# A two-layer MoE backbone: the selection of further blocks cut into pieces, and the first block without a list written as straight code under a condition

## The chip, the cores and the metric

The kernel runs on one core of a Trainium2 chip, as one launch. The metric is device time in microseconds (us) of a whole execution. TensorE is called PE here, its weight loads PEld, VectorE DVE, ScalarE ACT, GpSimd POOL, and SyncE, which issues nearly all weight loads, SP.

## What is computed

A backbone of two layers over 512 latent tokens of 1024 numbers with 256 context tokens beside them. Layer 0 mixes tokens by latent attention, layer 1 by a short gated convolution; a mixture of experts (MoE) follows each. Its core, cut to what matters:

```python
# 32 experts in 4 groups, 2 experts a token, 512 hidden numbers an expert
g_sel  = argmax(softmax(h @ w_group) + b_group)               # a group for each token
top_idx = top_k(softmax(logits of the group) + bias, 2)       # two experts in it
...
yp = lax.map(expert_block, (blocks of tokens of one expert, their expert))
def expert_block(xb, e):
    return (silu(xb @ w_gate[e]) * (xb @ w_up[e])) @ w_down[e]
return segment_sum(yp[dest] * weight, token)
```

How many tokens an expert gets depends on the data. All weights are fp32 and come from HBM: 6 MB an expert, 32 experts, two layers.

## The kernel before, in words

`moe()` (L583) runs once for each layer. Tokens are handled in blocks of 64 (`SLOTS`). There are 36 `LISTS`: the first 64 tokens of each of the 32 experts, and `FURTHER` = 4 further blocks, the next 64 tokens of those experts that have more than 64. Which expert a further block belongs to is known only at run time. `count_further()` (L711) counts on DVE how many further blocks each expert has (`nov`), where its first one stands (`first`), and their sum (`novi`); `select()` (L728) finds for `n` further blocks the expert (`own`, an integer that SP reads later), the place of each token in the block (`pos`) and three columns of its routing weight (`r`). Blocks beyond those four are handled by `beyond()` (L758): a loop `For_i(FURTHER, nv)` (L764) whose bounds every engine reads from memory. In this data it runs once in layer 0 and not at all in layer 1.

An expert `e` is, on PE: `gate_up` (L658, 32 matmuls, all of 64 tokens), the transposes `h_T` (L671), `down` (L681, 16 matmuls). Between the matmuls of `gate_up` stand the matmuls of `combine` (L698) of the expert before: eight of them, each followed by an add on DVE into the token tiles (L700). `fetch` (L642) transposes token rows of a later pair of experts there too. On the other engines: silu on ACT (L664) and times up on DVE (L665); `weighted` (L684) multiplies the expert's output by the routing weight on DVE (L686), makes the one-hot matrix `ohs` (L690), and splits the product into a high part (ACT, L688 and L689) and a low part (POOL L691, DVE L692). `combine` multiplies these with `ohs`. The rows of a block come by an indirect DMA on POOL (L635), from row numbers that a small matmul (L620, `table`) picks with a one-hot tile `pt` (L608, `onehot`); for the lists this is done for a pair of experts, two pairs ahead.

Each engine goes through its own instructions in program order, and the order follows the loop over `e` at L839. SP issues the loads in that order too: four blocks of gate and up weights (L302, 1 MB each) run 13 blocks ahead, the two `down` blocks (L315, 1 MB each) three experts ahead, and each load waits until its buffer is free. After expert 34 and before expert 35 the kernel combines expert 34 in one go and calls `beyond()`; expert 35 has no combine within it. `ahead(0..2)` issue the loads of the convolution's weights (L1527) in layer 0.

Of the kernel before, what the change touches and what calls it, by code (L numbers as in the profile page):

```python
# [87 lines left out]
def backbone(ctx: ExitStack, tc: tile.TileContext, A, out):  # L88
# [494 lines left out]
    def moe(l, x, big, normed, weights, gain, start, step, ahead=lambda i: None):  # L583


        with ExitStack() as st:
# [123 lines left out]

            def count_further():  # L711

                th = wide_[:, 256:256 + STEPS]
                cmp = wide_[:, :EXPERTS * STEPS].rearrange("p (e s) -> p e s", s=STEPS)
                dve.tensor_scalar(th, iota[:, :STEPS], float(SLOTS), float(SLOTS), op0=ALU.mult, op1=ALU.add)
                dve.tensor_tensor(cmp, cnt.unsqueeze(2).to_broadcast([P, EXPERTS, STEPS]),
                                  th.unsqueeze(1).to_broadcast([P, EXPERTS, STEPS]), op=ALU.is_gt)
                dve.memset(sc[:, 32:128], 0.0)
                dve.tensor_reduce(nov, cmp, axis=AX, op=ALU.add)
# [1 line left out]
                dve.tensor_copy(a[:, 16:], nov)
                for d in (1, 2, 4, 8, 16):
                    dve.tensor_add(b[:, 16:], a[:, 16:], a[:, 16 - d:48 - d])
                    a, b = b, a
                dve.tensor_sub(first, a[:, 16:], nov)
                dve.tensor_copy(novi, a[:1, 47:48])

            def select(ks, n, pos, r, own):  # L728


                d = sc[:, 160:160 + n * EXPERTS].rearrange("p (k e) -> p k e", e=EXPERTS)
                m = wide_[:, 256:256 + n * EXPERTS].rearrange("p (k e) -> p k e", e=EXPERTS)
                f = sc[:, 224:224 + n]
                prod = wide_[:, :4 * n * EXPERTS].rearrange("p (t k e) -> p t k e", t=4, e=EXPERTS)
                full = [P, n, EXPERTS]
                dve.tensor_tensor(d, ks.unsqueeze(2).to_broadcast(full), first.unsqueeze(1).to_broadcast(full), op=ALU.subtract)
                dve.tensor_tensor(m, d, nov.unsqueeze(1).to_broadcast(full), op=ALU.is_lt)
                dve.scalar_tensor_tensor(m, d, 0.0, m, op0=ALU.is_ge, op1=ALU.mult)
                dve.tensor_mul(d, d, m)
                dve.tensor_reduce(f, d, axis=AX, op=ALU.add)  # L740
                dve.tensor_scalar(f, f, float(SLOTS), SLOTS + 1.0, op0=ALU.mult, op1=ALU.add)
                dve.tensor_mul(d, m, iota[:, :EXPERTS].unsqueeze(1).to_broadcast(full))
                g = sc[:, 228:228 + n]
                dve.tensor_reduce(g, d, axis=AX, op=ALU.add)
                dve.tensor_copy(own, g[:1])
                for t in range(4):
                    dve.scalar_tensor_tensor(prod[:, t], posm[:, t, :].unsqueeze(1).to_broadcast(full), 1.0, m,
                                             op0=ALU.add, op1=ALU.mult)
                dve.tensor_reduce(pos, prod, axis=AX, op=ALU.add)
                for t in range(4):  # L750
                    dve.tensor_sub(pos[:, t], pos[:, t], f)
                for c in range(2, NTAB):
                    for t in range(4):
                        dve.tensor_mul(prod[:, t], R[:, t, :, c].unsqueeze(1).to_broadcast(full), m)
                    dve.tensor_reduce(g4 := sc[:, 160:160 + 4 * n].rearrange("p (t k) -> p t k", t=4), prod, axis=AX, op=ALU.add)
                    dve.tensor_copy(r[:, :, :, c], g4)

            def beyond():  # L758

                k, pos = cur[:, :1], cur[:, 4:8].rearrange("p (t k) -> p t k", k=1)  # L760
                dve.memset(k, FURTHER - 1.0)
                dve.tensor_copy(rc[:, :, 0], R[:, :, 0])
                nv = nc.values_load(novi[0:1, 0:1], min_val=0, max_val=2 * STEPS)
                with tc.For_i(FURTHER, nv, 1):  # L764
                    e = LISTS
                    dve.tensor_scalar_add(k, k, 1.0)
                    select(k, 1, pos, rc, owner[:, FURTHER:])
                    whose[l, e] = nc.values_load(owner[0:1, FURTHER:FURTHER + 1], engines=(mybir.EngineType.SP,),
                                                 min_val=0, max_val=EXPERTS - 1)
                    for i in range(4):  # L770
                        gate_block(l, e, i, big(f"gx{l}_{i}"))
                    load_down(l, e, big)
                    pt = onehot(pos, 0, 1, "x")
                    table(pt, rc, 1, LISTS, "x")
                    gather(LISTS // 2, (LISTS, LISTS), xgs[0])
                    v = xgs[0].rearrange("s (p j) -> s j p", j=8)
                    xTo = wide_.rearrange("p (j s) -> p j s", s=SLOTS)
                    for h in range(2):
                        tx = psum.tile([P, 4, SLOTS], F32, tag=("o", "xt")[h], name=f"tx{l}_{h}")
                        for j in range(4):  # L780
                            pe.transpose(tx[:, j], v[:64, 4 * h + j, :], ident[:64, :64])
                        for j in range(4):
                            act.activation(xTo[:, 4 * h + j, :], tx[:, j], AF.Identity, bias=mcol[:, l, 3, 0, 4 * h + j:4 * h + j + 1],
                                           scale=mcol[:, l, 4, 0, 4 * h + j:4 * h + j + 1])
                    gu = psum.tile([P, 512], F32, tag="gu", name=f"gux{l}")
                    gate_up(xTo, e, gu, {})
                    h_T("x")
                    y = psum.tile([P, 512], F32, tag="y", name=f"yx{l}")
                    down(e, y)
# [918 lines left out]
```

## Time and profile before

| what | us |
|---|---|
| three runs | 1911.83, 1905.15, 1909.97 |
| their median | 1909.97 |
| the profiled execution, whole | 1906.3 |
| its span (first to last instruction) | 1904.5 |
| mean clock granted to PE in it, as a share of full speed | 0.951 |
| DVE busy | 1151.3 |
| ACT busy | 580.6 |
| POOL busy | 368.3 |

The span lies 1.8 us below the time of the same execution, and that execution 3.7 us below the median of the runs. Times within the execution are counted from the span's start. "Layer 0" in what follows is its MoE, roughly 440 to 1050 us, and "layer 1" its MoE, roughly 1320 to 1895 us.

### The profile page before, as it was taken

The numbers are of one execution on the slowest core, as the hardware profiler recorded it, in microseconds if no ns is written. First come the engines' busy times: TensorE is split into PE (matmuls) and PEld (weight loads), VectorE is DVE, ScalarE is ACT, GpSimd is POOL, SyncE is SP. The second block draws the span as 40 slices with busy tenths as digits, with TensorE's granted clock in tenths as the row PEclk, the third lists the DMA queues.
The fourth block names the chain that finished last, engine by engine and source line by source line (L and its number), as shares of the span: only waits on it lengthen the run. The fifth ranks groups of instructions, "written<-read, shape, count | busy, mean of one in ns | idle before, by whom it ended". The sixth has DMA issues, their size and how long they took to land. (4 is left out here: it accounts for less than half of the span.)

```text
span 1904.5 us, 23932 instructions
## 1 busy us (share of the span) xinstructions
PE 1740.9 (91%) x8686; PEld 928.5 (49%) x8686; DVE 1151.3 (60%) x2339; ACT 580.6 (30%) x1329; POOL 368.3 (19%) x308
## 2 busy tenths in 40 slices
PE   5989999998889999999967999997988999999995
PEld 2878887863333333333322888873333333333331
DVE  4767787564665566555552776644666655566554
ACT  3455655221212222222211422222212222222222
POOL 0436666200100111101100321210101010111101
PEclk9999999998989999999987999998999999999996
DMA  9124334578989999999973473458999999999991
GB/s 342 55 99 153 130 120 155 208 310 313 417 334 410 417 417 416 416 416 417 416 296 146 146 247 108 133 205 327 417 364 359 416 416 417 416 417 416 417 382 56
DMA packets 139703, 574.24 MB, mean 302 GB/s; under 512 B 21184, under 2 KB 23488, under 8 KB 100928
## 3 DMA queue, kind: packets, MB, share of 16 engines
q1 hardware_dynamic: 132816, 549.09, 73.2%
q0 software_dynamic: 5328, 19.40, 2.6%
q10 hardware_dynamic: 1440, 4.20, 0.6%
q8 instruction: 70, 1.15, 0.2%
q14 instruction: 49, 0.40, 0.1%
HBM read 566.36 MB, written 6.29 MB: 301 GB/s over the span
## 5 line engine op out<-in xcount | busy, mean ns | idle before, releaser
L658 PE MATMUL gu<-gu,mA 128*64 128x512 f32 x2304 | 553.9, 614 | 3.5 <-issue 2.1
L700 DVE TENSOR_TENSOR xb<-xb,c 128x512 f32<-128x512 f32 x576 | 362.7, 682 | 61.0 <-PE c L698 58.1
L658 PEld LDWEIGHTS gu<-gu,mA 128*64 128x64 f32 x2304 | 154.4, 140 | 293.3 <-issue 290.8
L691 POOL TENSOR_TENSOR yst<-mB,yst 64x512 fp32r<-64x512 f32 x70 | 88.5, 1265 | 918.9 <-ACT yst L688 918.9
L681 PE MATMUL y<-d,mB 128*64 128x512 f32 x1152 | 263.1, 598 | 0.0
L698 PE MATMUL c<-yst,ohs 128*128 128x512 f32 x576 | 222.0, 468 | 34.3 <-DVE xb L700 23.2
L664 ACT ACTIVATE mB<-gu 64x256 f32<-64x256 f32 x144 | 54.4, 377 | 612.0 <-PE gu L658 576.7
L698 PEld LDWEIGHTS c<-yst,ohs 128*128 128x128 f32 x576 | 102.0, 195 | 171.9 <-DVE xb L700 89.9
L686 DVE SCALAR_TENSOR_TENSOR mB<-y,tab,mB 128x512 f32<-128x512 f32 x72 | 54.1, 751 | 204.6 <-PE y L681 204.6
L665 DVE TENSOR_TENSOR mB<-mB,gu 64x256 f32<-64x256 f32 x144 | 60.9, 423 | 144.0 <-ACT mB L664 144.0
L681 PEld LDWEIGHTS y<-d,mB 128*64 128x64 f32 x1152 | 76.3, 136 | 128.2 <-issue 123.3
L692 DVE TENSOR_TENSOR yst<-mB,yst 64x512 fp32r<-64x512 f32 x73 | 91.8, 1258 | 65.3 <-ACT yst L689 64.3
L647 ACT ACTIVATE mA<-xt,mcol 128x128 f32<-128x128 f32 x280 | 105.5, 457 | 24.1 <-issue 22.4
L688 ACT CAST yst<-mB 64x512 fp32r<-64x512 f32 x73 | 45.2, 620 | 196.4 <-DVE mB L686 196.4
L113 PE MATMUL bcu<-a1H,wis 128*128 128x512 f32 (+1 forms) x216 | 83.1, 385 | 0.0
L114 PE MATMUL bcu<-a1L,wis 128*128 128x512 f32 (+1 forms) x216 | 82.2, 381 | 0.0
L115 PE MATMUL bcu<-a1H,wis 128*128 128x512 f32 (+1 forms) x216 | 82.1, 380 | 0.0
L642 PEld LDWEIGHTS xt<-kc,xg 128*128 128x128 f32 x288 | 38.9, 196 | 73.5 <-issue 58.9
L671 PE MATMUL htp<-kc,mB 64*128 64x64 f32 x288 | 46.1, 240 | 28.2 <-DVE mB L665 19.3
L635 POOL DMA_INDIRECT xg<-normed,rows x37 | 36.1, 975 | 177.3 <-DVE rows L634 73.3
L109 POOL TENSOR_TENSOR wis<-wi,wis 128x512 fp32r<-128x512 f32 x26 | 39.6, 1531 | 151.6 <-ACT wis L108 149.0
L642 PE MATMUL xt<-kc,xg 128*128 128x128 f32 x288 | 52.9, 310 | 13.7 <-DMA xg<-normed,rows 13.7
(544 smaller groups left out, 2616.8 us busy)
## 6 DMA issues: line engine op xcount, KB each, us to landing
d<-in_moe_w_down_dram SPq DMA_DIRECT2D x146, 1024.0 KB, 14.4
gu<-in_moe_w_gate_dram SPq DMA_DIRECT2D x144, 1024.0 KB, 15.3
gu<-in_moe_w_up_dram SPq DMA_DIRECT2D x144, 1024.0 KB, 13.5
wm<-in_w_mod_dram SPq DMA_DIRECT2D x48, 1024.0 KB, 6.1
wi<-in_conv_w_in_dram SPq DMA_DIRECT2D x12, 1024.0 KB, 7.2
wo<-in_mla_w_o_dram SPq DMA_DIRECT2D x4, 1024.0 KB, 6.5
normed<-xn ACTq DMA_DIRECT2D x8, 512.0 KB, 4.7
wo<-in_conv_w_out_dram SPq DMA_DIRECT2D x4, 1024.0 KB, 5.0
```

The lines of the kernel that those rows point to most:

```text
L113: pe.matmul(o, ah, bh, start=first, stop=False)
L114: pe.matmul(o, ah, bl, start=False, stop=False)
L115: pe.matmul(o, al, bh, start=False, stop=last)
L642: pe.transpose(xt[:, j - js[0], :], v[:, j, :], ident)
L647: act.activation(xTs[b % 2][:, j], xt[:, j - js[0], :], AF.Identity, bias=mcol[:, l, 3, 0, j:j + 1], scale=mcol[:, l, 4, 0, j:j + 1])
L658: pe.matmul(gu[64 * s:64 * s + 64, :], xT[:, j, :], gates[l, e, j // 4 * 2 + s][:, j % 4, :], start=j == 0, stop=j == 7, tile_position=(0, ...
L665: dve.tensor_mul(ys[:64, cs], ys[:64, cs], gu[64:, cs])
L681: pe.matmul(y[64 * h:64 * h + 64, :], hT[:, k * 64:(k + 1) * 64], d[k // 2][:, k % 2, 512 * h:512 * h + 512], start=k == 0, stop=k == 3, t ...
L691: lo_engine.tensor_sub(y0[64:], ys[:64], y0[:64].bitcast(F32))
L692: dve.tensor_sub(y1[:64], ys[64:], y1[64:].bitcast(F32))
L698: pe.matmul(cps, ohs[:, t * P:(t + 1) * P], yst[:, h], start=True, stop=True)
L700: dve.tensor_add(xs, xs, cps)
```

## The change

- The selection is cut into 17 pieces: `counted` and `placed` (from `count_further`), then five pieces of `select` for each pair of further blocks and for one block more, the first without a list. Each expert from 2 to 18 runs one of them, after its combine and before its `down`.
- That one block more (number `FURTHER`) is selected always. Its expert is read by SP at `e` = 26, its row table and gather are made at `e` = 32 (`next_rows("a")`), and its 6 MB of weights are loaded at `e` = 33 (`next_weights`), in both layers and whether it has tokens or not.
- `beyond()` now tests `nv > FURTHER` (L818 of the changed kernel). Under the condition stands `block("a")`: the combine of expert 34, the block's transposes, `gate_up`, `h_T`, `down` and `weighted`. A loop for still further blocks follows within the condition, with the selection and loads of each as before.
- The combine of the last of these (or of expert 34, if the condition fails) is done within expert 35, as in every other expert.
- `ahead(0)` and `ahead(1)` move by one place each.

The diff, with the bodies that only got a name left out:

```diff
             def count_further():
...
+                return [counted, placed]
             def select(ks, n, pos, r, own):
...
+                def which():
...
+                def places():
...
+                def part(c):
...
+                return [which, places] + [lambda c=c: part(c) for c in range(2, NTAB)]
+
+            kx, posn = cur[:, :1], cur[:, 4:8].rearrange("p (t k) -> p t k", k=1)
+
+            def next_block():
+                return select(kx, 1, posn, rc, owner[:, FURTHER:])
+
+            def next_expert():
+                whose[l, LISTS] = nc.values_load(owner[0:1, FURTHER:FURTHER + 1], engines=(mybir.EngineType.SP,),
+                                                 min_val=0, max_val=EXPERTS - 1)
+            spare = []
+
+            def next_weights():
+                for i in range(4):
+                    gate_block(l, LISTS, i, spare[i])
+                left = spare[4:]
+                load_down(l, LISTS, lambda name: left.pop(0))
+
+            def next_rows(tag):
+                table(onehot(posn, 0, 1, tag), rc, 1, LISTS, tag)
+                gather(LISTS // 2, (LISTS, LISTS), xgs[0])
+
+            def block(tag):
+                combine(range(8), f"x{tag}")
...
+                weighted(y, tab[:, LISTS], dve)
 
             def beyond():
...
-                with tc.For_i(FURTHER, nv, 1):
...
-                    weighted(y, tab[:, LISTS], dve)
-                    combine(range(8), "x")
+                with tc.If(nv > FURTHER):
+                    block("a")
+                    with tc.For_i(FURTHER + 1, nv, 1):
+                        dve.tensor_scalar_add(kx, kx, 1.0)
+                        for f in next_block():
+                            f()
+                        next_expert()
+                        next_weights()
+                        next_rows("x")
+                        block("b")
...
-                if 0 < e < LISTS - 1:
+                if e:
                     between[3] = lambda: combine(range(3), f"{e - 1}")
...
-                within = 0 < e < LISTS - 1
+                within = e > 0
...
                 evac()
+                if e > 1 and few:
+                    few.pop(0)()
                 down(e, y)
 
+            few = count_further()
+            for k in range(0, FURTHER, 2):
+                ks = slice(k, k + 2)
+                few += select(iota[:, ks], 2, posx[:, :, ks], Rx[:, :, ks], owner[:, ks])
+            dve.memset(kx, float(FURTHER))
+            dve.tensor_copy(rc[:, :, 0], R[:, :, 0])
+            few += next_block()
             for e in range(LISTS):
...
-                if e == 2:
-                    count_further()
-                    dve.tensor_copy(Rx[:, :, :, :2], R[:, :, :FURTHER, :2])
-                if e in (4, 6):
-                    ks = slice(e - 4, e - 2)
-                    select(iota[:, ks], 2, posx[:, :, ks], Rx[:, :, ks], owner[:, ks])
...
+                    next_expert()
+                if e == LISTS - 4:
+                    next_rows("a")
                 if e == LISTS - 2:
-                    combine(range(8), e)
+                    ahead(0)
                     beyond()
+                    ahead(1)
...
-                if LISTS - 3 <= e < LISTS - 1:
-                    ahead(e - LISTS + 3)
+                if e == LISTS - 3:
+                    for i in range(4):
+                        spare.append(big(f"gx{l}_{i}") if i < 2 else ozblk(f"gx{l}_{i}", F32))
+                    spare.extend(wblk(f"dx{l}_{h}") for h in range(2))
+                    next_weights()
```

DVE at expert 4 of layer 0. Before (`xb` are the token tiles, `c0_3` the combine of expert 3, `y0_4` the output of expert 4, `mB` a tile that holds scratch):

```order
L700 TENSOR_TENSOR xb1_3290<-xb1_3290,c0_3_7_4452 128x512
L686 SCALAR_TENSOR_TENSOR mB0_3874<-y0_4_4398,tab0_3877,mB0_3874 128x512
L690 TENSOR_SCALAR ohs0_3876<-kc_86,tab0_3877 128x512
L692 TENSOR_TENSOR yst0_3875<-mB0_3874,yst0_3875 64x512
L624 TENSOR_REDUCE tab0_3877<-tb0_b4c0_4476 128x2
L625 TENSOR_SCALAR tab0_3877<-tab0_3877 128x2
L627 TENSOR_REDUCE tab0_3877<-tb0_b4c0_4476 128x2
L634 TENSOR_SCALAR rows0_3878<-tab0_3877 64x1 x2
L736 TENSOR_TENSOR mB0_3874<-kc_86,mB0_3874 128x64
```

and in the changed kernel:

```order
L700 TENSOR_TENSOR xb1_3290<-xb1_3290,c0_3_7_4454 128x512
L748 TENSOR_TENSOR mB0_3874<-kc_86,mB0_3874 128x64
L749 TENSOR_TENSOR mB0_3874<-mB0_3874 128x64
L750 SCALAR_TENSOR_TENSOR mB0_3874<-mB0_3874 128x64
L751 TENSOR_TENSOR mB0_3874<-mB0_3874 128x64
L752 TENSOR_REDUCE mB0_3874<-mB0_3874 128x2
L753 TENSOR_SCALAR mB0_3874<-mB0_3874 128x2
L754 TENSOR_TENSOR mB0_3874<-mB0_3874,kc_86 128x64
L755 TENSOR_REDUCE mB0_3874<-mB0_3874 128x2
L756 CAST owner0_3884<-mB0_3874 1x2
L686 SCALAR_TENSOR_TENSOR mB0_3874<-y0_4_4400,tab0_3877,mB0_3874 128x512
L690 TENSOR_SCALAR ohs0_3876<-kc_86,tab0_3877 128x512
```

The selection began (L736) behind `weighted` of expert 4 and went on with all its instructions; now the first piece, `which`, stands between the last add of the combine and `weighted`, and the other pieces are with later experts.

DVE at expert 32 of layer 0. Before:

```order
L686 SCALAR_TENSOR_TENSOR mB0_3874<-y0_32_7324,tab0_3877,mB0_3874 128x512
L690 TENSOR_SCALAR ohs0_3876<-kc_86,tab0_3877 128x512
L692 TENSOR_TENSOR yst0_3875<-mB0_3874,yst0_3875 64x512
L700 TENSOR_TENSOR xb0_3289<-xb0_3289,c0_32_0_7416 128x512
L700 TENSOR_TENSOR xb0_3289<-xb0_3289,c0_32_1_7419 128x512
```

and in the changed kernel (`pt0_a` is the one-hot tile, `tb0_a` the table that PE makes from it, right behind the `down` of expert 32 and ahead of the `gate_up` of expert 33):

```order
L686 SCALAR_TENSOR_TENSOR mB0_3874<-y0_32_7372,tab0_3877,mB0_3874 128x512
L690 TENSOR_SCALAR ohs0_3876<-kc_86,tab0_3877 128x512
L692 TENSOR_TENSOR yst0_3875<-mB0_3874,yst0_3875 64x512
L608 TENSOR_TENSOR pt0_a_7448<-cur0_3880,kc_86 128x256
L624 TENSOR_REDUCE tab0_3877<-tb0_a_7450 128x1
L625 TENSOR_SCALAR tab0_3877<-tab0_3877 128x1
L627 TENSOR_REDUCE tab0_3877<-tb0_a_7450 128x1
L634 TENSOR_SCALAR rows0_3878<-tab0_3877 64x1 x2
L700 TENSOR_TENSOR xb0_3289<-xb0_3289,c0_32_0_7481 128x512
```

Five rows are new between `weighted` and the adds; the first of them stands behind all of `weighted`.

PE around the condition, layer 0. Before:

```order
L681 MATMUL y0_34_7490<-d0_34_1_7322,mB0_3874 64x512 x4
L698 MATMUL c0_34_0_7557<-yst0_3875,ohs0_3876 128x512
L698 MATMUL c0_34_1_7560<-yst0_3875,ohs0_3876 128x512
L698 MATMUL c0_34_2_7563<-yst0_3875,ohs0_3876 128x512
L698 MATMUL c0_34_3_7566<-yst0_3875,ohs0_3876 128x512
L698 MATMUL c0_34_4_7569<-yst0_3875,ohs0_3876 128x512
L698 MATMUL c0_34_5_7572<-yst0_3875,ohs0_3876 128x512
L698 MATMUL c0_34_6_7575<-yst0_3875,ohs0_3876 128x512
L698 MATMUL c0_34_7_7578<-yst0_3875,ohs0_3876 128x512
L763 TENSOR_LOAD novi_103
L764 COMPARE_AND_BRANCH
```

and in the changed kernel:

```order
L681 MATMUL y0_34_7563<-d0_34_1_7370,mB0_3874 64x512 x4
L817 TENSOR_LOAD novi_103
L818 COMPARE_AND_BRANCH
L698 MATMUL c0_xa_0_7649<-yst0_3875,ohs0_3876 128x512
L698 MATMUL c0_xa_1_7652<-yst0_3875,ohs0_3876 128x512
```

The read of the count and the branch stood behind the combine of expert 34; now they stand ahead of it, and the combine is under the condition.

## Rows read from the trace of the kernel before

**Rows 1.** The page's line of busy time by engine (share of the span, number of instructions).

```profile
PE 1740.9 (91%) x8686; PEld 928.5 (49%) x8686; DVE 1151.3 (60%) x2339; ACT 580.6 (30%) x1329; POOL 368.3 (19%) x308
```

**Rows 2.** The timeline of DVE, the rows of `weighted` (L686): start, length, operation, and in brackets the idle time of DVE before it and what ended it. First four of layer 0 (experts 2, 8, 9, 10), then two of layer 1 (experts 2 and 8).

```profile
482.16 0.75 DVE L686 SCALAR_TENSOR_TENSOR mB<-y,tab,mB 128x512 f32<-128x512 f32 x1 [2.77 <-PE y L681]
...
589.74 0.75 DVE L686 SCALAR_TENSOR_TENSOR mB<-y,tab,mB 128x512 f32<-128x512 f32 x1 [2.77 <-PE y L681]
604.84 0.75 DVE L686 SCALAR_TENSOR_TENSOR mB<-y,tab,mB 128x512 f32<-128x512 f32 x1 [2.77 <-PE y L681]
619.66 0.75 DVE L686 SCALAR_TENSOR_TENSOR mB<-y,tab,mB 128x512 f32<-128x512 f32 x1 [2.77 <-PE y L681]
...
1360.96 0.75 DVE L686 SCALAR_TENSOR_TENSOR mB<-y,tab,mB 128x512 f32<-128x512 f32 x1 [2.77 <-PE y L681]
...
1470.00 0.75 DVE L686 SCALAR_TENSOR_TENSOR mB<-y,tab,mB 128x512 f32<-128x512 f32 x1 [2.77 <-PE y L681]
```

**Rows 3.** The timeline of DVE, layer 0: the first instruction of the count behind expert 2 (L715) and the add that follows it (L700); then, of the selection behind expert 4, the instruction with which each part begins (L736 which, L747 places, L754 the first and second of the three columns).

```profile
486.17 0.17 DVE L715 TENSOR_SCALAR mB<-kc 128x8 f32<-128x8 f32 x1
...
488.95 3.66 DVE L700 TENSOR_TENSOR xb<-xb,c 128x512 f32<-128x512 f32 x6
...
517.99 0.23 DVE L736 TENSOR_TENSOR mB<-kc,mB 128x64 f32<-128x64 f32 x1
...
519.96 0.61 DVE L747 SCALAR_TENSOR_TENSOR mB<-posm,mB 128x64 f32<-128x64 f32 x4
...
521.35 0.63 DVE L754 TENSOR_TENSOR mB<-R,mB 128x64 f32<-128x64 bf16 x4
...
522.55 0.62 DVE L754 TENSOR_TENSOR mB<-R,mB 128x64 f32<-128x64 bf16 x4
```

**Rows 4.** Windows: stretch, its length, busy time of PE, PEld, DVE, ACT and POOL (number of instructions), the clock granted to PE, share of the 16 DMA engines busy, GB/s. Within the selection, and behind it.

```profile
520.80:524.20 3.40, 0.00 (x0) 0.00 (x0) 3.23 (x21) 0.00 (x0) 0.00 (x0) 1.00 1.04 414
524.30:531.00 6.70, 5.34 (x11) 1.63 (x11) 4.23 (x9) 0.00 (x0) 0.00 (x0) 0.50 0.83 341
```

**Rows 5.** Windows, as above: the stretch of the selection and the experts after it in layer 0, and the selection's stretch in layer 1.

```profile
530.00:590.00 60.00, 53.41 (x256) 19.83 (x254) 35.48 (x87) 14.88 (x38) 4.76 (x4) 0.93 0.89 349
590.00:950.00 360.00, 352.06 (x1720) 131.88 (x1718) 214.14 (x385) 97.07 (x241) 41.79 (x36) 1.00 1.02 416
1400.00:1460.00 60.00, 48.64 (x206) 17.69 (x206) 38.43 (x112) 12.09 (x30) 4.76 (x4) 0.89 0.85 330
```

**Rows 6.** Time from issue to landing of the `down` blocks that are issued between 930 and 960 us, and the timeline of SP there: the last gate and up block of expert 34, and the two `down` blocks of expert 35.

```profile
DMA to landing us min/median/max: 20.0/20.0/20.1
...
934.91 0.33 SPq L302 DMA_DIRECT2D gu<-in_moe_w_up_dram  x1
...
952.46 3.42 SPq L315 DMA_DIRECT2D d<-in_moe_w_down_dram  x2
```

**Rows 7.** The timeline from expert 33 to expert 34 in layer 0, which are regular: the first `gate_up` load of expert 34, `weighted` of expert 33 (its first and last DVE instruction), the second half of that `gate_up`.

```profile
962.97 0.14 PEld L658 LDWEIGHTS gu<-gu,mA 128*64 128x64 f32 x2 [0.28 <-issue]
...
963.61 0.75 DVE L686 SCALAR_TENSOR_TENSOR mB<-y,tab,mB 128x512 f32<-128x512 f32 x1 [2.77 <-PE y L681]
...
965.69 1.28 DVE L692 TENSOR_TENSOR yst<-mB,yst 64x512 fp32r<-64x512 f32 x1 [0.93 <-ACT yst L689]
...
967.82 1.94 PE L658 MATMUL gu<-gu,mA 128*64 128x512 f32 x8
```

**Rows 8.** The timeline of the end of layer 0: `down` of expert 34, its combine, the one-hot tile and table of the further block, its transposes, `gate_up`, `down` and the last of its `weighted`, then expert 35's `gate_up` and `down`.

```profile
974.73 3.65 PE L681 MATMUL y<-d,mB 128*64 128x512 f32 x16
...
981.29 4.71 PE L698 MATMUL c<-yst,ohs 128*128 128x512 f32 x8 [2.91 <-POOL yst L691]
...
992.85 0.42 DVE L608 TENSOR_TENSOR pt_x<-cur,kc 128x256 bf16<-128x256 f32 x1
993.32 0.38 PE L620 MATMUL tb_x<-rc,pt_x 128*64 128x5 bf16 x8 [7.32 <-DVE pt_x L608]
...
1003.95 1.15 PE L781 MATMUL tx<-kc,xg 64*128 64x64 f32 x8 [10.25 <-DMA xg<-normed,rows]
...
1005.14 8.94 PE L658 MATMUL gux<-gx,mB 128*64 128x512 f32 x32
...
1016.29 3.65 PE L681 MATMUL yx<-d,mB 128*64 128x512 f32 x16
...
1022.15 0.69 DVE L692 TENSOR_TENSOR yst<-mB,yst 64x512 fp32r<-64x512 f32 x1
...
1028.45 9.23 PE L658 MATMUL gu<-gu,mA 128*64 128x512 f32 x32 [1.40 <-DVE xb L700]
...
1039.85 3.65 PE L681 MATMUL y<-d,mB 128*64 128x512 f32 x16
```

**Rows 9.** The same for layer 1, where the loop's body does not run: `down` of expert 34, the last of its `weighted`, its combine, expert 35's `gate_up` and `down`.

```profile
1855.30 3.65 PE L681 MATMUL y<-d,mB 128*64 128x512 f32 x16
...
1861.08 1.28 DVE L692 TENSOR_TENSOR yst<-mB,yst 64x512 fp32r<-64x512 f32 x1 [0.93 <-ACTq L764]
...
1861.86 4.71 PE L698 MATMUL c<-yst,ohs 128*128 128x512 f32 x8 [2.91 <-POOL yst L691]
...
1868.71 8.94 PE L658 MATMUL gu<-gu,mA 128*64 128x512 f32 x32 [2.14 <-issue]
...
1879.78 3.65 PE L681 MATMUL y<-d,mB 128*64 128x512 f32 x16
```

More of the change, by code (lines that the diff above doesn't have):

```diff
@@ L714, in count_further, with counted, placed @@
                 cmp = wide_[:, :EXPERTS * STEPS].rearrange("p (e s) -> p e s", s=STEPS)
[L715 to L719, printed above, removed]
-                a, b = sc[:, 32:80], sc[:, 80:128]
[L721 to L726, printed above, removed]
+                a, b = sc[:, 32:80], sc[:, 80:128]
+                def counted():
+                    dve.tensor_scalar(th, iota[:, :STEPS], float(SLOTS), float(SLOTS), op0=ALU.mult, op1=ALU.add)
+                    dve.tensor_tensor(cmp, cnt.unsqueeze(2).to_broadcast([P, EXPERTS, STEPS]),
+                                      th.unsqueeze(1).to_broadcast([P, EXPERTS, STEPS]), op=ALU.is_gt)
+                    dve.memset(sc[:, 32:128], 0.0)
+                    dve.tensor_reduce(nov, cmp, axis=AX, op=ALU.add)
+                def placed():
+                    u, v = a, b
+                    dve.tensor_copy(u[:, 16:], nov)
+                    for d in (1, 2, 4, 8, 16):
+                        dve.tensor_add(v[:, 16:], u[:, 16:], u[:, 16 - d:48 - d])
+                        u, v = v, u
+                    dve.tensor_sub(first, u[:, 16:], nov)
+                    dve.tensor_copy(novi, u[:1, 47:48])
+                    dve.tensor_copy(Rx[:, :, :, :2], R[:, :, :FURTHER, :2])
+                return [counted, placed]
             def select(ks, n, pos, r, own):
@@ L733, in select @@
                 f = sc[:, 224:224 + n]
+                g = sc[:, 228:228 + n]
+                g4 = sc[:, 160:160 + 4 * n].rearrange("p (t k) -> p t k", t=4)
                 prod = wide_[:, :4 * n * EXPERTS].rearrange("p (t k e) -> p t k e", t=4, e=EXPERTS)
                 full = [P, n, EXPERTS]
-                dve.tensor_tensor(d, ks.unsqueeze(2).to_broadcast(full), first.unsqueeze(1).to_broadcast(full), op=ALU.subtract)
-                dve.tensor_tensor(m, d, nov.unsqueeze(1).to_broadcast(full), op=ALU.is_lt)
@@ L738, in select @@
[L738 to L752, printed above, removed]
+                def which():
+                    dve.tensor_tensor(d, ks.unsqueeze(2).to_broadcast(full), first.unsqueeze(1).to_broadcast(full), op=ALU.subtract)
+                    dve.tensor_tensor(m, d, nov.unsqueeze(1).to_broadcast(full), op=ALU.is_lt)
+                    dve.scalar_tensor_tensor(m, d, 0.0, m, op0=ALU.is_ge, op1=ALU.mult)
+                    dve.tensor_mul(d, d, m)
+                    dve.tensor_reduce(f, d, axis=AX, op=ALU.add)
+                    dve.tensor_scalar(f, f, float(SLOTS), SLOTS + 1.0, op0=ALU.mult, op1=ALU.add)
+                    dve.tensor_mul(d, m, iota[:, :EXPERTS].unsqueeze(1).to_broadcast(full))
+                    dve.tensor_reduce(g, d, axis=AX, op=ALU.add)
+                    dve.tensor_copy(own, g[:1])
@@ L753, in select @@
+                def places():
+                    for t in range(4):
+                        dve.scalar_tensor_tensor(prod[:, t], posm[:, t, :].unsqueeze(1).to_broadcast(full), 1.0, m,
+                                                 op0=ALU.add, op1=ALU.mult)
+                    dve.tensor_reduce(pos, prod, axis=AX, op=ALU.add)
+                    for t in range(4):
+                        dve.tensor_sub(pos[:, t], pos[:, t], f)
+                def part(c):
                     for t in range(4):
@@ L754, in select @@
                         dve.tensor_mul(prod[:, t], R[:, t, :, c].unsqueeze(1).to_broadcast(full), m)
[L755 removed]
+                    dve.tensor_reduce(g4, prod, axis=AX, op=ALU.add)
                     dve.tensor_copy(r[:, :, :, c], g4)
+                return [which, places] + [lambda c=c: part(c) for c in range(2, NTAB)]
+            kx, posn = cur[:, :1], cur[:, 4:8].rearrange("p (t k) -> p t k", k=1)
@@ new lines, in next_rows @@
+            def next_rows(tag):
[3 more added lines that the diff above has]
+                combine(range(8), f"x{tag}")
+                v = xgs[0].rearrange("s (p j) -> s j p", j=8)
+                xTo = wide_.rearrange("p (j s) -> p j s", s=SLOTS)
+                for h in range(2):
+                    tx = psum.tile([P, 4, SLOTS], F32, tag=("o", "xt")[h], name=f"tx{l}_{tag}{h}")
+                    for j in range(4):
+                        pe.transpose(tx[:, j], v[:64, 4 * h + j, :], ident[:64, :64])
+                    for j in range(4):
+                        act.activation(xTo[:, 4 * h + j, :], tx[:, j], AF.Identity, bias=mcol[:, l, 3, 0, 4 * h + j:4 * h + j + 1],
+                                       scale=mcol[:, l, 4, 0, 4 * h + j:4 * h + j + 1])
+                gu = psum.tile([P, 512], F32, tag="gu", name=f"gux{l}{tag}")
+                gate_up(xTo, LISTS, gu, {})
+                h_T(f"x{tag}")
+                y = psum.tile([P, 512], F32, tag="y", name=f"yx{l}{tag}")
+                down(LISTS, y)
+                weighted(y, tab[:, LISTS], dve)
@@ L758, in beyond @@
             def beyond():
-                k, pos = cur[:, :1], cur[:, 4:8].rearrange("p (t k) -> p t k", k=1)
-                dve.memset(k, FURTHER - 1.0)
-                dve.tensor_copy(rc[:, :, 0], R[:, :, 0])
                 nv = nc.values_load(novi[0:1, 0:1], min_val=0, max_val=2 * STEPS)
-                with tc.For_i(FURTHER, nv, 1):
[L765 to L789, printed above, removed]
-                    weighted(y, tab[:, LISTS], dve)
-                    combine(range(8), "x")
```

## The prediction

> **What bounds the kernel now.** I read the page's busy line first [rows 1]. PE is busy for 91% of the span and nothing else for more than 60%, so the kernel is an almost unbroken stream of matmuls, and an edit can win only where PE stands still or runs at its lower clock, or lose by making such places. I then went along the start times of `weighted`, one for each expert, as a pulse [rows 2]. From expert 8 to 9 it is 15.10 us, from 9 to 10 it is 14.82 us: 29.92 us for two regular experts. Where the pulse is longer, PE lost time. The windows tell what loads do meanwhile [rows 5], and the timelines of the two ends what lies between expert 34 and 35 [rows 8, 9].
>
> **1. The selection leaves the path.** Six regular experts take 3 x 29.92 = 89.76 us. From expert 2 to 8, layer 0 takes 589.74 - 482.16 = 107.58 and layer 1 1470.00 - 1360.96 = 109.04 us [rows 2]. The excess, 17.8 and 19.3 us, is the count and two selections: they stand on DVE ahead of the adds of the next combine, whose three result buffers fill up, and PE stands still. [...]
>
> Now one piece for each expert stands ahead of `weighted`. There DVE is idle for 2.77 us, waiting for `down`, in every row shown [rows 2]. The longest piece, `which`, takes 519.96 - 517.99 = 1.97 us, `places` 1.39, a column 1.20; the whole count with its copy 488.95 - 486.17 = 2.78 us, and it is cut in two [rows 3]. Every piece fits with at least 0.8 us to spare, so I cost the pieces at nothing; their cover is `down`, and without it a piece delays `weighted` and the combine behind it (rival C). Gain: **17.8 + 19.3 = 37.1 us**. Nothing else is late in its place as long as the weights keep up; that is part 5.
>
> **2. The row table at expert 32: a new wait, in both layers.** The one-hot tile stands behind all of `weighted`, and PE makes the table ahead of expert 33's `gate_up`. Experts 33 and 34 show what a regular passage looks like: the next `gate_up` begins at 962.97, while `weighted` ends at 965.69 + 1.28 = 966.97 [rows 7]. The tile takes 0.42 and the table 0.38 us, 0.47 us after the tile began [rows 8]; so the same passage would have `gate_up` at 966.97 + 0.47 + 0.38 = 967.8 instead of 962.97: 4.8 us later. PE stands still for some 3.9 us of it, as long as in the selection's window, after which the clock was at 0.50 [rows 4]. What that adds is not shown alone. The nearest row is the further block's `gate_up`, which ran behind a wait of 10.25 us: 8.94 us for 32 matmuls, where eight take 1.94 in a regular expert and 32 would take 7.8 [rows 7, 8]; that is 1.2 us. At most 16 matmuls take double, 3.9 us more; at least the clock stays, 0. I take 1.7, near the row, with a little for the combine's matmuls between. Cost: 6.5 us a layer (4.8 to 8.7), **13.0 us** in all. The four DVE instructions behind the table (0.7 us) and the gather on POOL go beside `gate_up`; the adds of the combine come later by no more than PE does.
>
> **3. The further block of layer 0.** Before, from `down` of expert 34 to `down` of expert 35 it is 1039.85 - 974.73 = 65.1 us [rows 8]. In it lie the combine, the selection, the tile and table, and 10.25 us in which PE waits for the gather; the weights were loaded in this time too. After the change, rows and weights are asked for two experts earlier. Then: combine ends at 981.29 + 4.71 = 986.0; transposes and their ACT copies take 1005.14 - 1003.95 = 1.2, so `gate_up` begins at 987.2; from there to `down` 1016.29 - 1005.14 = 11.15 (998.3); from `down` to the end of `weighted` 1022.15 + 0.69 - 1016.29 = 6.55 (1004.9). The combine of the block now lies within expert 35, which begins when the loop's test is done; I give that 1.1 us, less than the 1.40 us that PE stood before expert 35 [rows 8] (1006.0). From `gate_up` to `down` a regular expert with a combine takes 974.73 - 962.97 = 11.76 [rows 7, 8]; at the lower clock I add 2.5 (0 to 3.9 as in part 2, and more than there since PE comes from a longer stretch of short matmuls and waits). `down` of expert 35 is at 1006.0 + 11.76 + 2.5 = 1020.2, not 1039.85: **19.6 us** less (18.2 to 22.1).
>
> **4. The end of layer 1.** Here the condition fails. Before, the combine of expert 34 stood alone, and `gate_up` of 35 began at 1868.71, after 2.14 us in which PE waited for nothing that the profile shows [rows 9]; the read of the count and the branch fall there. After, both come right behind `down`, which ends at 1855.30 + 3.65 = 1858.95, and run beside `weighted`. PE goes on when DVE and ACT have reached the condition, so `gate_up` begins at 1861.08 + 1.28 + 0.4 = 1862.8, and `down` 11.76 + 2.5 later, at 1877.0 instead of 1879.78: **2.7 us** less (0 to 5). What I take for the branch is the 2.14 us shown, from 1858.95 to 1861.1, hidden behind `weighted`.
>
> **5. The loads.** They move into time that has been full. From 590 to 950 us the 16 DMA engines are busy without a gap (1.02, 416 GB/s), but in the stretch of the selections only at 0.89 and 0.85 [rows 5]: buffers came free late there. A load lands 20.0 us after its issue, so the last block of expert 34, issued at 934.91, is there at 954.9 and used from 967.82: 12.9 us in hand [rows 6, 7]. PE will come 17.8 us earlier. But the DMA gap closes too: (1.02 - 0.89) x 60 = 7.8 us. In hand: 12.9 - 17.8 + 7.8 = 2.9 us in layer 0, and 6.5 more after expert 32. In layer 1 the gap is (1.02 - 0.85) x 60 = 10.2 us against 19.3. So PE still waits for no load, by little. The block's six loads follow expert 35's `down` on SP. Before, that lands at 952.46 + 2.5 + 20.0 = 975.0 [rows 6]; with the gap closed at 967.2. At 2.51 us a block (1 MB at 416 GB/s) the first pair of gate and up is there at 972.2 and the last `down` block at 982.3, on before's time scale. PE wants them 17.8 - 6.5 = 11.3 us before the times of part 3: 987.2 - 11.3 = 975.9 and 998.3 - 11.3 = 987.0. Covered, by 3.7 and 4.7 us. In layer 1 these 6 MB are waste, but no engine but SP waits for them, and the last load of the kernel is small.
>
> **Sum.** -17.8 - 19.3 + 13.0 - 19.6 - 2.7 = -46.4 us. Against the profiled execution of 1906.3 us that is 1859.9. The median of the three runs stands 3.7 us above that execution, so I give **1862 us**. The bounds of parts 2 to 4, all at one end, are 3.4 + 2.5 + 2.5 = 8.4 us below and 4.4 + 1.4 + 2.7 = 8.5 us above: 1854 to 1871.
>
> **The rivals.**
> A. *The loads become the bound.* If the DMA engines do not win back the 7.8 and 10.2 us (the same buffers may hold them back), 12.9 - 17.8 = -4.9 us in layer 0, and with the same 12.9 in hand -6.4 in layer 1: PE waits so long, once in each, before expert 32; the block's loads then come 4.1 us late for a PE that is 4.9 later itself. For it: a queue busy at 1.02 for 360 us. Against: the gap is plainly there. 1862 + 11.3 = 1873 (1871 to 1875). 0.14.
> B. *Branches cost more than 2.14 us.* The code that a failing condition jumps over is now longer (the block and the loop's body), and at the loop's end PE jumps as well. If an engine must first fetch its instructions through DMA engines that are full, a jump may take as long as the gather took in the same place, at most 10.25 us [rows 8]. In layer 1 the branch starts at 1858.95, so 1858.95 + 10.25 is 6.4 us past my 1862.8; in layer 0 the loop's end would be up to 9 us later. With a quarter to all of these 15.4: 1866 to 1877. Against: before's jump cost at most the 2.14 us [rows 9], though with few loads under way. 0.16.
> [...]
> C. *The pieces are not hidden: slower.* If a piece outlasts DVE's idle time, or waits for something that `down` waits for too, `weighted` comes late, the next combine too, and PE stands still and drops to half clock, as the selection showed. The count alone, 2.8 us of DVE, cost part of 17.8; three such stalls cost 17.8, some 3 to 6 us each. 17 pieces in two layers at 3 us are 102 us, in place of the 37 gained: about 1960. It decides where a piece passes 2.77 us. Against: the longest is 1.97. 0.03.
> D. *The change does not do what it says*: the block's weights are not there in time, or `block("a")` does not run in layer 0. Before ran the loop once, so `nv` is 5 and the condition holds; the loads are asked for 20 us ahead. 0.01, with a time near A's.
>
> **How the numbers follow.** My forecast 0.66, A 0.14, B 0.16, C 0.03, D 0.01. Forecast, A and most of B lie between 1849 (1854, and 5 less by the 3.7 us that I added for the median and 1.3 us of rounding) and 1874; outside are C, the top of B and A, and a tail of the forecast: under 2 in 10. Runs of this kernel agree within 0.3%, 5.7 us, and less than that can't be told from no change. Forecast, A, B and D are all faster than 1904.2, so faster 0.96, slower 0.03 (C), same 0.01.
>
> **What would show it.** Right: the pulse at 14.8 and 15.1 us from expert 2 to 8 too, with a piece in front of each `weighted` and DVE still idle before it; a gap 5 to 8 us longer once, behind expert 32, and the clock at 0.50 after it; DMA share 1.02 from 500 us on without the dip; from `down` of 34 to `down` of 35 about 45.5 us in layer 0 and 21.8 in layer 1. Wrong: PE waiting for DMA in `gate_up` late in the lists or in the block (A); idle PE behind `down` of 34 or at the loop's end without a releaser (B); idle PE ahead of combines from expert 2 to 18 (C).

## The result

The changed kernel takes 1862.04 us (median of 4 runs, 1861.40 to 1866.88) where the kernel before takes 1910.54 (4 runs, 1905.15 to 1911.83): a ratio of 0.9757, 95% interval 0.9734 to 0.9780. The forecast was 1862. The profiled execution takes 1861.4 us, its span 1859.6. One of the four runs of e1 below took 2436.95 us at a granted clock of 0.647, where its others have 0.952 to 0.960, and is left out of e1's figures.

The page's busy line, as [rows 1]: PE works 7 us less in a span that is 45 us shorter.

```profile
PE 1733.5 (93%) x8694; PEld 929.0 (50%) x8694; DVE 1161.1 (62%) x2380; ACT 580.3 (31%) x1329; POOL 369.0 (20%) x309
```

The starts of `weighted` in the changed kernel, as [rows 2] (experts 2, 3, 4 and 8 of layer 0, then 2 and 8 of layer 1):

```profile
486.80 0.75 DVE L686 SCALAR_TENSOR_TENSOR mB<-y,tab,mB 128x512 f32<-128x512 f32 x1 [1.77 <-PE y L681]
501.90 0.75 DVE L686 SCALAR_TENSOR_TENSOR mB<-y,tab,mB 128x512 f32<-128x512 f32 x1 [1.17 <-PE y L681]
516.72 0.75 DVE L686 SCALAR_TENSOR_TENSOR mB<-y,tab,mB 128x512 f32<-128x512 f32 x1 [0.82 <-PE y L681]
...
576.56 0.75 DVE L686 SCALAR_TENSOR_TENSOR mB<-y,tab,mB 128x512 f32<-128x512 f32 x1 [1.55 <-PE y L681]
...
1333.67 0.75 DVE L686 SCALAR_TENSOR_TENSOR mB<-y,tab,mB 128x512 f32<-128x512 f32 x1 [1.77 <-PE y L681]
...
1423.43 0.75 DVE L686 SCALAR_TENSOR_TENSOR mB<-y,tab,mB 128x512 f32<-128x512 f32 x1 [1.55 <-PE y L681]
```

From expert 2 to 8 both layers take 89.76 us, to the hundredth the three regular pairs of part 1. The idle time in brackets, 2.77 us without a piece, shows what is left of it: 0.82 with the longest. The windows of the same stretch, as [rows 4, 5]: full clock (1.00), and the loads without a dip (1.02).

```profile
500.00:560.00 60.00, 58.68 (x292) 22.10 (x290) 41.49 (x98) 16.19 (x41) 6.97 (x6) 1.00 1.02 415
...
939.40:946.00 6.60, 6.56 (x25) 2.12 (x26) 0.65 (x5) 0.00 (x0) 0.95 (x1) 0.60 1.01 416
```

The second window is that behind expert 32, where the mean granted clock is 0.60. PE there, as [rows 7], shows what went before: it waits 3.89 us for the one-hot tile, and 16 matmuls that one expert earlier take 3.60 us (first row) take 6.11.

```profile
920.57 3.60 PE L658 MATMUL gu<-gu,mA 128*64 128x512 f32 x16
...
931.90 3.65 PE L681 MATMUL y<-d,mB 128*64 128x512 f32 x16
939.44 0.38 PE L620 MATMUL tb_a<-rc,pt_a 128*64 128x5 bf16 x8 [3.89 <-DVE pt_a L608]
939.67 6.11 PE L658 MATMUL gu<-gu,mA 128*64 128x512 f32 x16
```

The end of layer 0, as [rows 8], and of layer 1, as [rows 9]; the gather's 10.25 us is gone, and what PE waits for last is the loop's test (L820) in layer 0 and the condition (L818) in layer 1:

```profile
968.31 3.65 PE L681 MATMUL y<-d,mB 128*64 128x512 f32 x16
974.87 4.77 PE L698 MATMUL c_xa<-yst,ohs 128*128 128x512 f32 x8 [2.91 <-POOL yst L691]
...
980.77 9.49 PE L658 MATMUL gux0a<-gx,mB 128*64 128x512 f32 x32
...
992.49 5.32 PE L681 MATMUL yx0a<-dx,mB 128*64 128x512 f32 x16
1001.42 5.35 PE L658 MATMUL gu<-gu,mA 128*64 128x512 f32 x16 [3.61 <-DVEq L820]
...
1814.37 3.65 PE L681 MATMUL y<-d,mB 128*64 128x512 f32 x16
1821.73 5.35 PE L658 MATMUL gu<-gu,mA 128*64 128x512 f32 x16 [3.71 <-DVEq L818]
```

### The profile page after: what moved, and what is told of

Its sections match the earlier page's. It is cut to its first block, busy times and chain, and to the rows that moved or that the text cites. A ratio compares the mean times of both kernels' runs of the same rounds, so it can differ in the third digit from the quotient of the medians.

```text
span 1859.6 us, 24009 instructions
## 1 busy us (share of the span) xinstructions
PE 1733.5 (93%) x8694; PEld 929.0 (50%) x8694; DVE 1161.1 (62%) x2380; ACT 580.3 (31%) x1329; POOL 369.0 (20%) x309
## 3 DMA queue, kind: packets, MB, share of 16 engines
HBM read 573.18 MB, written 6.29 MB: 312 GB/s over the span
## 5 line engine op out<-in xcount | busy, mean ns | idle before, releaser
L700 DVE TENSOR_TENSOR xb<-xb,c 128x512 f32<-128x512 f32 x576 | 363.2, 683 | 89.5 <-PE c L698 86.5
L698 PE MATMUL c<-yst,ohs 128*128 128x512 f32 x576 | 212.1, 449 | 4.9 <-DVE yst L691 4.4
L698 PEld LDWEIGHTS c<-yst,ohs 128*128 128x128 f32 x576 | 97.9, 189 | 138.3 <-DVE xb L700 62.5
L686 DVE SCALAR_TENSOR_TENSOR mB<-y,tab,mB 128x512 f32<-128x512 f32 x72 | 54.1, 751 | 157.4 <-PE y L681 157.4
L217 POOL TENSOR_TENSOR wacc<-wacc,wm 128x512 f32<-128x512 f32 x42 | 55.0, 1309 | 45.9 <-ACT wacc L211 23.0
```

Of the source, the lines that this page charges most:

```text
L217: pool.tensor_add(wacc, wacc, w)
L698: pe.matmul(cps, ohs[:, t * P:(t + 1) * P], yst[:, h], start=True, stop=True)
L700: dve.tensor_add(xs, xs, cps)
```

## The experiments

All intervals below are differences between starts of `weighted` in the profiled execution (layer 0 / layer 1, us): from expert 2 to 8, from 32 to 33, and from 34 to 35, the last with all that lies around the condition. The ratio is to the kernel before on the same chip, with its 95% interval.

| kernel | ratio | 2 to 8 | 32 to 33 | 34 to 35 |
|---|---|---|---|---|
| before | | 107.58 / 109.04 | 14.79 / 14.82 | 65.12 / 24.48 |
| changed | 0.9757 (0.9734 to 0.9780) | 89.76 / 89.76 | 21.62 / 20.75 | 46.28 / 20.51 |
| e1 pieces alone | 0.9840 (0.9791 to 0.9889) | 89.76 / 89.76 | 14.79 / 14.82 | 66.14 / 25.69 |
| e2 one-hot early | 0.9718 (0.9676 to 0.9759) | 89.78 / 89.78 | 14.98 / 14.97 | 46.81 / 21.67 |
| e3 pieces behind | 0.9865 (0.9825 to 0.9905) | 93.72 / 93.84 | 20.55 / 21.67 | 45.24 / 20.36 |
| e4 whole, ahead | 0.9897 (0.9855 to 0.9939) | 102.64 / 102.59 | 20.75 / 20.75 | 46.38 / 20.42 |
| e5 not crossing | 0.9818 (0.9770 to 0.9867) | 89.78 / 89.77 | 21.74 / 21.76 | 45.65 / 28.37 |
| e6 no block in layer 1 | 0.9679 (0.9633 to 0.9725) | 89.76 / 89.77 | 21.77 / 14.79 | 43.06 / 14.79 |
| e7 early, and clock | 0.9691 (0.9646 to 0.9736) | 89.78 / 89.78 | 14.98 / 14.98 | 51.03 / 18.85 |
| e8 the same, weights first | 0.9729 (0.9669 to 0.9789) | 89.78 / 89.78 | 14.98 / 14.98 | 44.28 / 25.18 |
| e9 e5, shifted by 48 | one execution | 89.78 / 89.78 | 21.58 / 21.69 | 52.64 / 25.91 |
| e10 e5, shifted by 20 | one execution | 89.78 / 89.78 | 21.87 / 21.80 | 45.67 / 28.34 |
| e11 e2, weights first | 0.9735 (0.9692 to 0.9778) | 89.77 / 89.79 | 14.98 / 14.98 | 45.28 / 25.29 |
| e12 e7, weights first in layer 0 | 0.9666 (0.9638 to 0.9694) | 89.78 / 89.78 | 14.98 / 14.98 | 43.40 / 18.86 |

**e1, the pieces alone.** The kernel before, with `count_further` and `select` of the change and

```diff
+                if e > 1 and few:
+                    few.pop(0)()
                 down(e, y)
```

> The kernel before with the selection of the four further blocks cut into 12 pieces, one ahead of weighted in each expert from 2 to 13; the loop for blocks beyond, with its selection, rows and weights, stays as it was. Theory: the excess of 17.8 and 19.3 us goes and nothing else changes: the pulse is 14.8 and 15.1 us from expert 2 to 8, from down of 34 to down of 35 stays 65.1 and 24.5 us, and the time is 1910.5 - 37.1 = 1873. Rival (a gain that the loads take back): PE waits for weights late in the lists, 1880 to 1890.

Measured: both excesses are gone whole, and the ends stay within 1.2 us of what they were. The time, 1873.38 us (median of three runs), is a gain of 21 to 40 us by the interval of the ratio. So the selection is a term of its own, as the sum has it.

**e3 and e4: is it the cut, or the place?** In e3 the piece is run behind `weighted` instead of ahead of `down`; in e4 the pieces run ahead of `down`, but together. The edit of e4:

```diff
-                if e > 1 and few:
-                    few.pop(0)()
+                for _ in range({2: 2, 4: 5, 6: 5, 8: 5}.get(e, 0)):
+                    few.pop(0)()
```

> The changed kernel with each of the 17 pieces behind weighted of its expert, where the whole selection stood before, instead of ahead of it. Theory A (the cut is what counts: three result buffers and 0.5 to 0.9 us of idle DVE behind each group of adds absorb a piece under 2 us): at most 0.6 us for each of the longest pieces, 1862 to 1866. Theory B (the place is what counts: behind weighted DVE is on the path, as it was when 16.7 us of DVE cost 17.8 us): 22.3 us of pieces a layer cost some 24, 1862 + 47 = 1909.

> The changed kernel with the selection uncut, at the new place: the whole count ahead of weighted of expert 2, a whole pair (7.0 us of DVE) ahead of experts 4 and 6, the further block (5.6 us) ahead of expert 8. Theory: idle DVE of 2.77 us covers that much of each and no more; 4.2 + 4.2 + 2.8 us come through, and some 1.8 us of slow matmuls behind each: 16.6 us a layer, 1862 + 33 = 1895. Rival (the place alone hides all of it): 1862. Other rival (nothing is hidden once a piece is too long): 1862 + 2 x 25 = 1912.

e3 came between its theories (1880.40 us): from expert 2 to 19 it takes 263.93 us in layer 0, the changed kernel 254.46, so 17 pieces cost 9.5 us, none more than 1.4. The trace shows how: the adds begin once the piece is through, and each of the next three combine matmuls waits for the result buffer that an add gives back.

```profile
526.22 0.23 DVE L748 TENSOR_TENSOR mB<-kc,mB 128x64 f32<-128x64 f32 x1
...
528.18 3.65 DVE L700 TENSOR_TENSOR xb<-xb,c 128x512 f32<-128x512 f32 x6
```

```profile
528.91 1.70 PE L698 MATMUL c<-yst,ohs 128*128 128x512 f32 x3 [0.27 <-DVE xb L700]
529.50 0.19 PEld L698 LDWEIGHTS c<-yst,ohs 128*128 128x128 f32 x1 [0.41 <-DVE xb L700]
530.10 0.19 PEld L698 LDWEIGHTS c<-yst,ohs 128*128 128x128 f32 x1 [0.41 <-DVE xb L700]
```

Three of these matmuls take 0.96 us undisturbed. The buffers absorb about half of a piece, not all of it as theory A had it. In e4 the interval that ends at expert 4 grows by 4.09 us, the 4.2 us by which a pair outlasts the idle DVE, and the next one by 1.20 us; the count costs nothing, the single block 2.74 and 1.13. That is the theory's mechanism with a smaller bill for the slow matmuls behind each: 14.0 us a layer where I had 16.6. Place and cut both count: the gap ahead of `weighted` hides 2.77 us and no more.

**e2, the one-hot tile early.**

```diff
+                pta = onehot(posn, 0, 1, "a") if e == LISTS - 4 else None
                 expert(e, y)
...
-                    next_rows("a")
+                    table(pta, rc, 1, LISTS, "a")
+                    gather(LISTS // 2, (LISTS, LISTS), xgs[0])
```

> The changed kernel with the one-hot tile of the further block made ahead of expert 32 instead of behind its weighted; the table on PE stays where it is. Theory: the table no longer waits, and the gaps of 6.8 and 5.9 us behind expert 32 go (to 0.2 us). But the block's weights land 4.5 us before they are used, so PE will wait some 2.2 us for them in layer 0: gain 4.6 + 5.7 = 10.3 us, 1852. Rival 1 (weights have more cover than that): 1849.5. Rival 2 (the gap comes from the table, its gather or the clock, not from the tile's place): 1860 to 1862.

The wait at expert 32 is gone but for 0.2 us, so it was the tile's place. The block's `gate_up` now starts, and after two matmuls waits 1.22 us for weights, where 2.2 were expected from their cover:

```profile
971.78 1.07 PE L658 MATMUL gux0a<-gx,mB 128*64 128x512 f32 x2
974.07 8.70 PE L658 MATMUL gux0a<-gx,mB 128*64 128x512 f32 x30 [1.22 <-DMA gx<-in_moe_w_up_dram]
```

So the first rival fails by this row; the time, 1849.44 us, could not have told it from the theory. The interval around the condition grew by 0.5 us in layer 0, since the block's `down` ran faster this time (3.65 us against 5.32), and by 1.2 us in layer 1, where 16 matmuls of expert 35's `gate_up` took 6.46 us against 5.35.

**e5 and e6: what the condition is worth.** e5 takes the crossing out (`combine(range(8), e)` ahead of `beyond()`, the block's combine at its own end, `if 0 < e < LISTS - 1` in `expert`); e6 puts `if l == 0` ahead of `next_rows`, `beyond` and `next_weights`.

> The changed kernel with no combine across the condition: expert 34 is combined in one go ahead of it, the block under the condition at its own end, and expert 35 has no combine within it, as before the change. Theory: rows and weights that are there early make the gain in layer 0, crossing only the end in layer 1. Layer 1 from down of 34 to down of 35 goes back from 20.5 to about 24.5 us (+4.0), layer 0 from 46.3 to about 48.6 (the block's combine of 4.9 us alone against 2.6 within an expert): 1862 + 6.3 = 1868. Rival (crossing is what made layer 0 shorter): layer 0 goes to 55 to 65 us, 1875 to 1885.

> The changed kernel, with the further block left out in layer 1 (where this data has none): no row table, no 6 MB of weights, no condition there. Theory: the gap behind expert 32 (5.9 us) goes, and expert 35 follows 34 at the regular 14.8 us instead of 20.5: -5.9 - 5.7 = -11.6, 1850.5; the weights not loaded give nothing. Rival (the branch itself is cheap and the wait before expert 35 is one for weighted in any case): -5.9 and 20.5 us stay, 1856. Other rival (the 6 MB delay loads that PE waits for): a gain over 12 us.

e5: in layer 0 its 45.65 us look like no gain from the crossing (46.28 with it), but the block's matmuls ran faster in e5: 7.09 and 3.65 us for `gate_up` and `down`, against 9.49 and 5.32. In e6, where layer 0 is that of the changed kernel, crossing included, the block ran at e5's speed, and the interval is 43.06 (first row e5, second e6):

```profile
979.38 7.09 PE L658 MATMUL gux0a<-gx,mB 128*64 128x512 f32 x32
```

```profile
982.15 7.09 PE L658 MATMUL gux0a<-gx,mB 128*64 128x512 f32 x32
```

So the crossing is worth about 2.6 us in layer 0, near the 2.3 expected, and rows and weights that are there early made most of the 19 us. In layer 1 leaving the crossing out costs 7.9 us, twice what I expected, and 3.9 more than the kernel before took. The trace names the reason: PE waits for its own sequencer, whose branch takes 6.03 us.

```profile
1834.32 8.83 PE L658 MATMUL gu<-gu,mA 128*64 128x512 f32 x32 [6.29 <-PEq L818]
```

```profile
L818 PEldq COMPARE_BRANCH  x2: 92/3058/6025, 978.1 to 1827.9; - x2
```

(Shortest, median and longest of the two layers, in ns.) The changed kernel has such a branch too:

```profile
L818 PEldq COMPARE_BRANCH  x2: 92/2655/5218, 969.3 to 1815.2; - x2
```

There it begins at 1815.23, beside `down` and `weighted`, and ends at 1820.45, 1.3 us before `gate_up` of 35. e6 saves 6.0 us at expert 32 and 5.7 at 35 in layer 1, as theory had it; the weights it doesn't load add nothing. Its time, 1846.98 us, lies below the 1850.5 expected; in layer 0, whose code is unchanged, the interval around the condition was 3.2 us shorter.

**e9 and e10: is the branch long wherever it stands?** In e5 it took 6.03 us of an interval of 28.37; the longest of the kernel before took 0.33, and so short a branch would leave 22.7. Only the start of layer 1 differs from e5:

```diff
-            keep_clock(psum, "gu", 12, f"e{l}")
+            keep_clock(psum, "gu", 12 + 24 * l, f"e{l}")
```

and 10 instead of 24 in e10. Each such matmul takes two places, with its weight load, so what follows moves by 48 places in e9 and by 20 in e10. Places are counted in the built program.

> The run without a combine across the condition, and 24 more matmuls that nothing reads at the start of layer 1's MoE, which moves everything behind them by 48 places in PE's instruction stream. [...]

> [...] Theory: the branch takes 5 to 6 us and 28.4 us stay. Rival (the added matmuls themselves, or any shift, change the branch): under 0.5 us, 22.7.

```profile
L818 PEldq COMPARE_BRANCH  x2: 92/226/359, 985.1 to 1838.1; - x2
```

```profile
L818 PEldq COMPARE_BRANCH  x2: 92/2935/5778, 982.7 to 1832.8; - x2
```

First e9, then e10: 0.36 us and 5.78 us, for the same jump over the same code. In e9 `gate_up` of 35 follows the combine after 1.26 us, in e10 after 6.15, though the interval shrinks by 2.4 us only, as PE then ran `gate_up` and `down` of 35 slower (9.47 and 5.30 us against 8.94 and 3.65 in e10): 25.9 us, not 22.7. The layer 0 interval of e9 is 7 us longer than e10's with unchanged code, 3.8 of it between the first branches of L818 and L820 on PE (985.1 to 1009.6 against 982.7 to 1003.4).

**e7, e8, e11, e12: a version that beats both.** e7 is e2 with matmuls that nothing reads in PE's waits; e8 and e11 move `load_down(l, LISTS - 1)` behind `next_weights()`, e12 does so in layer 0 only.

```diff
                 weighted(y, tab[:, LISTS], dve)
+                keep_clock(psum, "gu", 14, f"b{l}{tag}")
...
+                    keep_clock(psum, "gu", 12, f"w{l}")
                     ahead(0)
                     beyond()
```

> The changed kernel with the one-hot tile early as in the run with that alone, and with matmuls that nothing reads, 12 ahead of the condition and 14 behind the down of the further block, where PE stands for 2.9 to 3.7 us. Theory: they keep the clock at full speed, and gate_up of 35 saves some 1.7 us in each layer; in layer 0 the block's own gate_up saves nothing, since it waits for weights: 1852 - 3.4 = 1848.5. Rival (the wait, not the clock, is all): 1852. Other rival (the matmuls delay what PE waits for): 1853 to 1856.

> The kernel with the one-hot tile early and the matmuls that nothing reads, and the further block's six loads ahead of the two down loads of expert 35 on SP, not behind them. Theory (in layer 0 the block's gate_up waited for weights once the wait at expert 32 was gone, 12.4 us for 32 matmuls with these matmuls and 11.0 without): the weights land some 5 us sooner, gate_up takes 7.1 to 8.9 us, and from down of 34 to down of 35 in layer 0 it is 44 to 47 us instead of 51.0; layer 1 keeps its 18.9: 1845. Rival (the clock, not the weights, made gate_up long): 50 to 51 us, 1849 to 1851. Other rival (the down loads of 35, now 15 us later, are waited for): layer 1 over 22 us.

> The kernel with the one-hot tile early, with the same order of loads and without the matmuls that nothing reads. Theory: gate_up of the block in layer 0 takes 7.1 to 9.5 us instead of 11.0, and from down of 34 to down of 35 it is 43 to 45.5 instead of 46.8; layer 1 keeps 21.7: 1847. Rival: 46.8 stays, 1849.5.

> The kernel with the one-hot tile early and the matmuls that nothing reads; the further block's six loads go ahead of the two down loads of expert 35 in layer 0 only, and behind them in layer 1, as in the changed kernel. Theory (in layer 0 the block waits for its weights, in layer 1 expert 35 waits for its down if that comes last): from down of 34 to down of 35, layer 0 takes 44.3 us as with the order changed in both layers, layer 1 18.9 as with it changed in neither. Against the changed kernel that is 6.6 + 5.8 us at expert 32, 2.0 and 1.7 us at the ends: 1862 - 16 = 1846, a ratio to before of 0.968. Rival: the two orders hang together (buffers are handed out in the order of the loads over both layers), and layer 1 is at 22 us or more.

e7: in layer 1 it saves 2.8 us against e2, where 1.7 were expected, all in 16 matmuls of `gate_up` (3.65 us against 6.46); in layer 0 the block waits for weights and then runs slowly (12.43 us), a miss. e8 and e11 mend that (7.09 and 8.85 us) and lose it in layer 1, where `down` of 35 now waits for its own load, as the second rival of e8 said: 25.2 and 25.3 us. Their times, 1859.24 and 1854.91 us, miss the 1845 and 1847 expected. e12 has both good halves, 43.40 and 18.86 us: 1841.41 us, its ratio 0.9666 (0.9638 to 0.9694) below all of the changed kernel's interval. The order in layer 0 suits this data, which has one block more there and none in layer 1.

## Why the prediction was right

Each term, forecast against measured in the profiled executions:

| part | forecast, us | measured, us |
|---|---|---|
| 1, selection (both layers) | -37.1 | -17.82 - 19.28 = -37.1 |
| 2, row table (layer 0 / 1) | +6.5 / +6.5 | +6.8 / +5.9 |
| 3, block in layer 0 | -19.6 | -18.8 |
| 4, end of layer 1 | -2.7 | -4.0 |
| sum | -46.4 | -47.2 |

The profiled executions differ by 44.9 us; the 2.3 us between lie nearly all in stretches that the change doesn't touch (the first `weighted` of layer 0 is 4.6 us later, the stretch between the two MoEs 2.0 us shorter).

Two rows of before, for parts 2 and 4:

```profile
963.39 3.60 PE L658 MATMUL gu<-gu,mA 128*64 128x512 f32 x16
```

```profile
L764 PEldq COMPARE_BRANCH  x6: 64/185/333, 985.9 to 1868.5; - x6
```

- Part 1 was exact because the excess could be read off a regular pulse, and e1 shows that it stands alone. e4 shows what bounds it: the 2.77 us. (Rival C's 3 to 6 us a stall do not fit that pulse: in layer 0 the count cost 1.9 us, the two selections 8.1 and 7.8.)
- Part 2: mechanism right (e2), and the sum near, but with one wrong reading. The working takes 962.97, a weight load, for the begin of `gate_up`; its first matmul is at 963.39 (first row above). So the wait was worth 4.4 us by its own working, not 4.8, and came as 4.3 and 4.2. The slow matmuls took 2.5 us in layer 0 (6.11 against 3.60) and 1.7 in layer 1 (5.33 against 3.60), where I had 1.7.
- Part 3: the block's `gate_up` began 12.46 us behind the start of `down` of 34, as worked out. `down` of the block ran slow (1.7 us that I did not have); its `gate_up` to `down` took 0.6 us more, while expert 35 followed 0.4 us sooner and took 1.1 us less from `gate_up` to `down` than I had: 0.4 by the reading above, 0.7 because the slow matmuls cost 1.8 us and not 2.5. Errors of both signs that nearly cancelled.
- Part 4: right in sign, 1.3 us short, nearly all of it the same 1.1 us. Its step on the branch was wrong: I took 2.14 us from before, and the branch took 5.22. The 2.14 us were no long branch either; a row of before tells (second row above): its longest branch on PE, the jump over the loop in layer 1, took 0.33 us, and the rest is 13 semaphore events of 0.05 us and two shorter branches on PE's sequencer, with the gaps between them. Rival B, which had 0.16, was right that a jump can take longer than 2.14 us; its price did not come because the branch is issued ahead of the wait for `weighted` (e5 puts it behind, and PE waits 6.29 us). That the time goes into a fetch through full DMA engines, as the rival supposes, is not shown.
- Part 5: the least time in hand before expert 33 is 5.4 us in layer 0, where I had 2.9; the block's first pair of weights lands 4.6 us before it is wanted (3.7 forecast). e2 used that up and waited.
- The total: that 1862 and 1862.04 agree so closely is luck. My own sum and the 3.7 us to the median give 1863.6, not 1862, and stretches that the change doesn't touch moved the profiled time by some 2 us.

The changed kernel's branch goes from place 17877 to 18207 of PE's stream and takes 5.22 us; e7's goes from 17981 to 18366, 55 places farther, and takes 0.37. e9 and e10 jump over the same code, from places that lie 28 apart, and take 0.36 and 5.78. So how far the branch goes does not alone set its length, and a shift of the code changes it; by what rule is not shown. Nor is it shown that a fetch takes the time: from 1815.20 to 1820.50 us, around the changed kernel's long branch, each of the two instruction queues of its profile (q8 and q14) moved one packet, beside loads that took 99.7% of the DMA engines; but from 1820.50 to 1825.00 they moved one and two.

## What to carry to other kernels

Work that is off the critical engine still costs if it stands between a result and its consumer: measure the idle gap ahead of each wait (2.77 us here), cut the work to fit it, and place it there. Put a data-dependent branch ahead of a wait that exists anyway, and look at the branch's own row, because here the same jump took 0.36 us in e9 and 5.78 in e10, with the code shifted. When a wait is removed, see which load becomes the next bound before its order is changed, in each layer by itself.

## What was not expected of the hardware

- The same taken branch on PE lasts 0.36 or 5.8 us, by a shift of 28 instructions (e9 against e10).
- The same code runs at different speed between executions: the block's 32 `gate_up` matmuls in layer 0, with their weights there, take 7.09 us in e6 and 9.49 in the changed kernel, at a mean granted clock of 0.74 (980.80 to 990.00 us). What sets it is open. Up to the first `weighted` of layer 0 the profiled executions lie between 450.6 (e4) and 463.5 us (e8), more than most edits here are worth, which is why the intervals and not the totals carry the argument.
